# The 32 bytes of swapped gate biases in another pool, and the read of the token count behind another expert's loads

## The chip, the cores and the metric

One core of a Trainium2 chip runs the kernel. The metric is device microseconds (us) of one execution, and lower is better. TensorE does the matrix products, VectorE (DVE), ScalarE (ACT) and GpSimd (POOL) the rest, and the queue of SyncE (SP) issues nearly all transfers from the memory outside the core; 16 DMA engines carry them.

## The reference, cut to what matters

One layer over 256 tokens of width 1024: a first half with normalization, convolution and recurrence, and a mixture of 32 experts, two for each token. All is float32.

```
    x = x + g1 * (concatenate([conv_l, lru_l]) @ w_out)
    h2 = modulate(rms_norm(x, norm2_g), sh2, sc2)
    y2 = hier_moe(h2, ...)          # top 1 of 4 groups, in it the top 2 of 8 experts
    x = x + g2 * y2
    return rms_norm(x, final_g)

def swiglu_expert(xb, w1, w3, w2):  # each expert, 1024x1024 weights, on its tokens
    return (silu(xb @ w1) * (xb @ w3)) @ w2
```

The kernel reads the weights of all 32 experts: 3 matrices of 4 MB each for an expert, 403 MB in all.

## The kernel before, in words

**The stages.** The first half of the layer (the prologue, lines 97 to 852) is an order written out by hand. It works in 17 tiles named slot, each 8192 bytes in a partition, in the pool `wp`. Behind it the pool is closed and the same bytes are taken again by nine tiles named wide, each 16,384 bytes in a partition (pool `wx`). One load fills a wide with half of a weight matrix of an expert, 2048 KB: line 885, called in `up`, with 128 rows of 16,384 contiguous bytes, one for each partition. So an expert takes six loads in the order w1, w1, w3, w3, w2, w2, and the loop `for e in range(E - 1)` runs over experts 0 to 30. Loads are counted here from 0: expert e has loads 6e to 6e+5. The nine wides are taken in a fixed turn, so load n goes into the wide that load n-9 had, and SP issues it when TensorE has done its products (line 888) with load n-9. Expert 31 is loaded in shorter rows, of 2048 bytes first (line 1070).

**What TensorE does for an expert.** Sixteen products for each load; between w3 and w2 four transposes (line 1015); behind odd experts' w3 the gather of tokens for the next group of experts (line 800), behind even experts' w3 the products that add the results of the pair before (line 910).

**The token count.** The tokens of an expert fit into 64 places, or, where some expert has more, a second piece of program (`rest`) runs at the end. For this, behind expert 1, VectorE and TensorE find the greatest count (lines 1042 to 1047, result in `fmi`), and `values_load` (line 1049) reads it into a register of every engine, so that each can decide at the end whether it runs the second piece. In SP's queue this read stands where the text has it: behind the loads of expert 2 and ahead of those of expert 3. SP executes its queue in order; the read waits for `fmi`, and everything behind it waits with it.

**The biases.** `hbx`, 8 floats in each partition (32 bytes), is a copy of biases with the two halves of the partitions swapped; the activations of the recurrence's gates read it (line 425), all in the prologue. It lies in the pool `const`, which lives to the end. The pools lie one behind the other: const, the one-hot tiles, the gathered tokens (xg), the slots, tmp, big. In the built program the first slot begins at byte 66,080 of a partition, and so does the first wide, 32 bytes past a multiple of 512; the others follow at multiples of 8192 or 16,384 from there. x1, the tile that holds the tokens, lies at the head of const and begins 128 bytes past a multiple of 512.

Of the kernel before, what the change touches and what calls it, by code (L numbers as in the profile page):

```python
# [7 lines left out]
F32 = mybir.dt.float32  # L8
# [62 lines left out]
def hybrid_layer(ctx: ExitStack, tc: tile.TileContext, sp_d, x_d, c_d, bada_d, rb_d, fg_d, gw_d,  # L71
# [5 lines left out]
    const = ctx.enter_context(tc.tile_pool(name="const", bufs=1))  # L77
# [5 lines left out]
    big = pro.enter_context(tc.tile_pool(name="big", bufs=1))  # L83
    psp = ctx.enter_context(tc.tile_pool(name="psp", bufs=8, space=bass.MemoryType.PSUM))

    def bank():
        return psp.tile([128, 512], F32, name="bank")
# [136 lines left out]
    V.tensor_scalar(nkh, kh, -1.0, None, OP.mult)  # L224
    hb = sp[:, COLS["ba"][0]:COLS["bx"][1]]
    V.tensor_scalar(hb, hb, 0.5, None, OP.mult)
    hbx = const.tile([128, 8], F32, name="hbx")
    for h in range(2):
        G.tensor_copy(hbx[64 * h:64 * h + 64], hb[64 - 64 * h:128 - 64 * h, 8:16])
    dwh = col("dw")  # L230
# [313 lines left out]
    def rowbc(dst, rows, j0):  # L544
        for j in range(2):
            pr = bank()
            r = 32 * (j0 + j)
            P.matmul(pr, ones[r:r + 1, :], rows[r:r + 1, :], start=True, stop=True, tile_position=(r, 0))
            S.copy(dst[:, j * 512:(j + 1) * 512], pr)
# [230 lines left out]
    def onehot(oh, t, g):  # L780
        V.tensor_tensor(oh[:, t], iota1[:, None, :].to_broadcast([128, 4, CAP]),
                        posm[:, t, g * 4:g * 4 + 4, None].to_broadcast([128, 4, CAP]), OP.is_equal)
# [12 lines left out]
    def quad(k):  # L795

        return slice(k // 4 * 512 + k % 4, k // 4 * 512 + 512, 4)

    def gather_mm(pg, i, k, oh, t):
        P.matmul(pg[:, i * 256:(i + 1) * 256], xn[:, t, quad(k)],  # L800
                 oh[:, t].rearrange("p e s -> p (e s)"), start=t + i == 0, stop=t == 1 and i == 1,
                 skip_group_check=True)

    def gather_out(xg, pg, i, k):
        if i == 0:
            S.activation(xg[:, k], pg[:, i * 256:(i + 1) * 256], AF.Identity, scale=gsp[:, 0, k:k + 1],  # L806
                         bias=gsp[:, 1, k:k + 1])
        else:
            V.tensor_scalar(xg[:, k], pg[:, i * 256:(i + 1) * 256], gsp[:, 0, k:k + 1], gsp[:, 1, k:k + 1],  # L809
                            OP.mult, OP.add)  # L810

    def gather_new(dt=F32):
        return (ohp.tile([128, 2, 4, CAP], dt, name="oh"),
                xgt().rearrange("p (k s) -> p k s", k=8))
# [66 lines left out]
    def up(w_d, e, xs):  # L881
        ps = bank()
        for k4 in range(2):
            w = wide().rearrange("p (k n) -> p k n", k=4)
            dma(w, w_d[e, k4 * 512:(k4 + 1) * 512, :].rearrange("(p k) n -> p k n", p=128))
            for i in range(4):
                for h in range(2):
                    P.matmul(ps[64 * h:64 * h + 64, :], xs(k4 * 4 + i), w[:, i, h * 512:(h + 1) * 512],  # L888
                             start=k4 + i == 0, stop=k4 * 4 + i == 7, tile_position=(0, 64 * h))
        return ps  # L890

    def sel_build(e0):
        so = mo.tile([128, 2, 2, CAP], F32, name="so")
        for t in range(2):
            for i in range(2):
                V.tensor_scalar(so[:, t, i], iota1, posm[:, t, e0 + i:e0 + i + 1],
                                gate[:, t, e0 + i:e0 + i + 1], OP.is_equal, OP.mult)
        return so

    def sel_turn(so):  # L900
        pt = bank()
        for t in range(2):
            P.transpose(pt[:, t * 128:(t + 1) * 128], so[:, t].rearrange("p e s -> p (e s)"), ident)
        st = mo.tile([128, 256], F32, name="st")
        S.copy(st, pt[:, 0:256])
        return st

    def scatter_mm(st, yy, t, h):
        pz = bank()
        P.matmul(pz, st[:, t * 128:(t + 1) * 128], yy[:, h * 512:(h + 1) * 512], start=True, stop=True)  # L910
        return pz

    def scatter_add(pz, t, h):
        q = slice(h * 512, (h + 1) * 512)
        V.tensor_tensor(x1[:, t, q], x1[:, t, q], pz, OP.add)  # L915
# [64 lines left out]
    for e in range(E - 1):  # L980
        xs = lambda k: xg[:, k, (e % 4) * CAP:(e % 4 + 1) * CAP]
        if e % 2 == 0:
            so = sel_build(e)
        gat = e % 2 == 1 and e // 4 < E // 4 - 1
        if gat and e % 4 == 1:
            noh, nxg = gather_new()
            onehot(noh, 0, e // 4 + 1)
            onehot(noh, 1, e // 4 + 1)
        pa = up(w1_d, e, xs)
        sl = mo.tile([128, 512], F32, name="sl", bufs=1)  # L990
        S.activation(sl, pa, AF.Silu)  # L991
        if e == 0:
            rowbc(g2bc, g2r, 2)
        if e % 2 == 0:
            st = sel_turn(so)
        pb = up(w3_d, e, xs)
        gg = sl
        V.tensor_tensor(gg, sl, pb, OP.mult)  # L998
        pzs = []
        k0 = (e % 4) // 2 * 4  # L1000
        if gat:
            pgs = [bank(), bank()]
            for k in range(3):
                for t in range(2):
                    gather_mm(pgs[k // 2], k % 2, k0 + k, noh, t)
            for k in range(2):
                gather_out(nxg, pgs[0], k, k0 + k)
        elif e % 2 == 0 and e:
            for n in range(3):
                pzs.append(scatter_mm(*prev, *TH[n]))  # L1010
                if n < 2:
                    scatter_add(pzs[n], *TH[n])
        pt = bank()
        for j in range(4):
            P.transpose(pt[:, j * 128:(j + 1) * 128], gg[:, quad(j)], ident)  # L1015
        gt = mo.tile([128, 4, 128], F32, name="gt", bufs=1)
        V.tensor_copy(gt[:, 0:2], pt[:, 0:256])  # L1017
        S.copy(gt[:, 2:4], pt[:, 256:512])  # L1018
        if gat:
            for t in range(2):  # L1020
                gather_mm(pgs[1], 1, k0 + 3, noh, t)
            for k in range(2, 4):
                gather_out(nxg, pgs[1], k % 2, k0 + k)
        elif pzs:
            pzs.append(scatter_mm(*prev, *TH[3]))
            for n in range(2, 4):
                scatter_add(pzs[n], *TH[n])
        gts = lambda f: gt[:, f % 4, 64 * (f // 4):64 * (f // 4) + 64]
        py = up(w2_d, e, gts)
        if e % 2 == 0:  # L1030
            yy = mo.tile([128, D], F32, name="yy", bufs=1)
        for h in range(2):
            o = (e % 2) * 64
            V.tensor_tensor(yy[o:o + 64, h * 512:(h + 1) * 512], py[64 * h:64 * h + 64, :],  # L1034
                            g2bc[64 * h:64 * h + 64, h * 512:(h + 1) * 512], OP.mult)
        if e % 2 == 1:
            prev = (st, yy)
        if e % 4 == 3:
            xg = nxg
        if e == 1:  # L1040
            fmx = mo.tile([128, 1], F32, name="fmx")
            V.tensor_reduce(fmx, posm.rearrange("p t e -> p (t e)"), AX.X, OP.max)
            fpt = bank()
            P.transpose(fpt[0:1, 0:128], fmx, ident)
            fmr = mo.tile([1, 1], F32, name="fmr")
            V.tensor_reduce(fmr, fpt[0:1, 0:128], AX.X, OP.max)
            V.tensor_copy(fmi, fmr)
        if e == 2:
            nmax = nc.values_load(fmi[0:1, 0:1], min_val=0, max_val=T)
        if e == 2:  # L1050
            dma(fgbc[0:1, :], fg_d)
            for j in range(2):
                pr = bank()
                P.matmul(pr, ones[0:1, :], fgbc[0:1, j * 512:(j + 1) * 512], start=True, stop=True)
                S.copy(fgbc[:, j * 512:(j + 1) * 512], pr)
# [8 lines left out]
    e = E - 1  # L1064
# [171 lines left out]
```

## Time and profile before

| what | value |
| --- | --- |
| median of 3 runs | 1135.12 us (1133.21 to 1136.87) |
| the profiled execution | 1132.48 us |
| its span, first to last instruction | 1130.6 us |
| mean granted TensorE clock, as a share of 2.4 GHz | 0.983 |
| bytes moved | 445.21 MB |

The profiled execution is 2.6 us under the median. Its span leaves 1.9 us around it.

### The profile page before, as it was taken

The page shows a single profiled execution, that of the slowest core. Times are in us where ns is not written, and L with a number is a line of the kernel's source. Part 1 is how long each engine was busy: PE and PEld are TensorE (multiplying, and loading weights), DVE is VectorE, ACT ScalarE, POOL GpSimd, SP SyncE. Part 2 cuts the span into 40 slices and gives each one's busy share as a digit, 9 for nine tenths or more (in the row PEclk, how much of TensorE's full clock was granted, in tenths as well). Part 3 has the DMA queues.
Part 4 walks back from the last instruction along what each step waited for, and adds up shares of the span by engine and source line. Part 5 has one row for each costly group of instructions (what it writes and reads, how often), then busy time and mean ns, then how long its engine had stood idle before and what let it go on. Part 6 is the DMA issues. An engine that isn't in the chain of part 4 may idle for free.

```text
span 1130.6 us, 11884 instructions
## 1 busy us (share of the span) xinstructions
PE 1002.3 (89%) x4959; PEld 445.6 (39%) x4959; DVE 312.8 (28%) x632; ACT 177.1 (16%) x331; POOL 97.8 (9%) x122
## 2 busy tenths in 40 slices
PE   6898898999999888988888898888988888888896
PEld 6874547343434332333333333332323333332244
DVE  4889965211121112111211121102121211111113
ACT  4558944100100000000000000000000000000002
POOL 2667412000000000000000000000000000000001
PEclk9999898999999999999999999999999999999999
DMA  9858668989999999999999999999999999999995
GB/s 347 300 202 325 233 258 375 403 353 429 427 427 426 426 427 427 428 426 427 427 427 426 427 428 427 427 427 428 427 427 426 427 427 428 425 428 427 428 392 183
DMA packets 50015, 445.21 MB, mean 394 GB/s; under 512 B 4083, under 2 KB 14371, under 8 KB 24100
## 3 DMA queue, kind: packets, MB, share of 16 engines
q1 hardware_dynamic: 49746, 443.84, 94.3%
q8 instruction: 41, 0.67, 0.2%
q10 hardware_dynamic: 210, 0.55, 0.1%
q14 instruction: 18, 0.15, 0.0%
HBM read 443.32 MB, written 1.05 MB: 393 GB/s over the span
## 4 chain that ended last, share of the span: by engine, by line
DMA 58%; PE 32%; DVE 6%; ACT 1%; SPq 1%; issue 1%; POOL 0%; DVEq 0%; ACTq 0%
DMA wide<-in_w_dram 57%; PE bank L888 17%; PE bank L800 3%; PE bank L691 2%; PE bank L910 2%; DVE bank L480 1%; PE bank L339 1%; PE bank L385 1%; PE bank L522 1%; DVE slot L394 1%; DMA slot<-in_wada_dram 1%; PE bank L826 1%; PE bank L323 1%; PE bank L1015 1%; DVE xn L480 1%; DVE slot L298 1%
## 5 line engine op out<-in xcount | busy, mean ns | idle before, releaser
L888 PE MATMUL bank<-wide,xg 128*64 128x512 f32 x1984 | 451.9, 600 | 83.2 <-DMA wide<-in_w_dram 82.9
L888 PEld LDWEIGHTS bank<-wide,xg 128*64 128x64 f32 x1984 | 142.0, 137 | 378.4 <-issue 257.5
L888 PE MATMUL bank<-wide,gt 128*64 128x512 f32 x992 | 219.7, 595 | 1.0 <-DVE gt L1017 1.0
L998 DVE TENSOR_TENSOR sl<-sl,bank 128x512 f32<-128x512 f32 x31 | 21.3, 687 | 476.7 <-issue 452.5
L888 PEld LDWEIGHTS bank<-wide,gt 128*64 128x64 f32 x992 | 68.5, 137 | 139.9 <-issue 138.5
L1034 DVE TENSOR_TENSOR yy<-bank,g2bc 64x512 f32<-64x512 f32 x62 | 42.7, 689 | 191.4 <-PE bank L888 190.9
L991 ACT ACTIVATE sl<-bank 128x512 f32<-128x512 f32 x31 | 18.5, 597 | 436.6 <-PE bank L888 436.6
L1153 POOL TENSOR_TENSOR xg<-x,fgbc 128x256 f32<-128x256 f32 x6 | 4.3, 730 | 924.2 <-DMA wide<-in_w_dram 923.0
L800 PE MATMUL bank<-oh,xn 128*128 128x256 f32 x224 | 61.1, 416 | 0.0
L800 PEld LDWEIGHTS bank<-oh,xn 128*128 128x128 f32 x224 | 54.4, 327 | 11.4 <-issue 11.4
L910 PE MATMUL bank<-yy,st 128*128 128x512 f32 x120 | 58.0, 606 | 0.0
L1018 ACT COPY gt<-bank 128x256 f32<-128x256 f32 x31 | 11.6, 373 | 226.0 <-DVE gt L1017 226.0
L806 ACT ACTIVATE xg<-bank,gsp 128x256 f32<-128x256 f32 x32 | 17.9, 565 | 154.7 <-PE bank L800 150.1
L915 DVE TENSOR_TENSOR x<-x,bank 128x512 f32<-128x512 f32 x60 | 39.7, 683 | 7.1 <-PE bank L910 7.1
L910 PEld LDWEIGHTS bank<-yy,st 128*128 128x128 f32 x120 | 20.6, 191 | 26.5 <-issue 23.2
L339 PE MATMUL bank<-slot 128*128 128x256 f32 x192 | 26.8, 301 | 4.3 <-DVE slot L298 4.3
L809 DVE TENSOR_SCALAR xg<-bank,gsp 128x256 f32<-128x256 f32 x32 | 17.2, 543 | 47.0 <-ACT xg L806 47.0
L339 PEld LDWEIGHTS bank<-slot 128*128 128x128 f32 x192 | 25.5, 206 | 5.6 <-DVE slot L298 4.8
L311 POOL TENSOR_TENSOR slot<-slot 128x512 fp32r<-128x512 f32 x20 | 26.5, 1358 | 9.3 <-ACT slot L302 9.3
L1015 PEld LDWEIGHTS bank<-ident,sl 128*128 128x128 f32 x124 | 19.5, 203 | 11.1 <-issue 7.1
L498 POOL TENSOR_TENSOR xn<-xn,fgbc 128x256 f32<-128x256 f32 x30 | 22.6, 753 | 13.0 <-ACT fgbc L497 8.4
L385 PE MATMUL bank<-slot 128*128 128x512 f32 x96 | 22.7, 394 | 0.0
(251 smaller groups left out, 694.1 us busy)
## 6 DMA issues: line engine op xcount, KB each, us to landing
wide<-in_w_dram SPq DMA_DIRECT2D x186, 2048.0 KB, 39.2
slot<-in_wada_dram SPq DMA_DIRECT2D x16, 1024.0 KB, 7.2
slot<-in_wada_dram SPq DMA_DIRECT2D x16, 512.0 KB, 9.3
slot<-in_win_dram SPq DMA_DIRECT2D x8, 1024.0 KB, 10.2
wide<-in_w_dram SPq DMA_DIRECT2D x8, 1024.0 KB, 24.0
slot<-in_wout_dram SPq DMA_DIRECT2D x4, 1024.0 KB, 9.4
wide<-in_w_dram SPq DMA_DIRECT2D x8, 512.0 KB, 12.5
x<-in_x_dram SPq DMA_DIRECT2D x2, 512.0 KB, 4.4
```

Source lines behind the costliest of these rows:

```text
L311: en.tensor_tensor(lo[:, c:c + m], w[:, c:c + m], f(hi)[:, c:c + m], OP.subtract)
L339: P.matmul(pvg[ct][:, i * T:(i + 1) * T], wz[k // 2][wi][:, k % 2, c:c + 128], x[k // 4][:, k % 4, 0:T], start=k + i + n == 0, stop=k == 7 ...
L385: P.matmul(pu, w, x[k // 4][:, k % 4], start=k + n == 0, stop=k == 7 and n == 2)
L480: V.scalar_tensor_tensor(rows4(ypre[:, ct]) if j == 30 else y, x, w, y, OP.mult, OP.add)
L498: G.tensor_tensor(acc, acc, p, OP.add)
L691: P.matmul(p, m[:, q], w[:, c:c + 512], start=first and n == 0, stop=len(done) == 8 and n == len(passes) - 1)
L800: P.matmul(pg[:, i * 256:(i + 1) * 256], xn[:, t, quad(k)], oh[:, t].rearrange("p e s -> p (e s)"), start=t + i == 0, stop=t == 1 and i == ...
L888: P.matmul(ps[64 * h:64 * h + 64, :], xs(k4 * 4 + i), w[:, i, h * 512:(h + 1) * 512], start=k4 + i == 0, stop=k4 * 4 + i == 7, tile_positi ...
L910: P.matmul(pz, st[:, t * 128:(t + 1) * 128], yy[:, h * 512:(h + 1) * 512], start=True, stop=True)
L915: V.tensor_tensor(x1[:, t, q], x1[:, t, q], pz, OP.add)
L1015: P.transpose(pt[:, j * 128:(j + 1) * 128], gg[:, quad(j)], ident)
L1034: V.tensor_tensor(yy[o:o + 64, h * 512:(h + 1) * 512], py[64 * h:64 * h + 64, :], g2bc[64 * h:64 * h + 64, h * 512:(h + 1) * 512], OP.mult)
```

## The change

Two edits. `hbx` goes from the pool const to the pool big, which lies behind the slots and tmp. All that stood behind it in const, and the pools behind const, move down by 32 bytes: the slots and the wides then begin at multiples of 512 (the first at byte 66,048); x1 stays where it was. And `values_load` is called in the round of expert 8 and no longer in that of expert 2; `fmi` is computed where it was.

```
-    hbx = const.tile([128, 8], F32, name="hbx")
+    hbx = big.tile([128, 8], F32, name="hbx")
...
-        if e == 2:
+        if e == 8:
             nmax = nc.values_load(fmi[0:1, 0:1], min_val=0, max_val=T)
         if e == 2:
             dma(fgbc[0:1, :], fg_d)
```

SP's queue before, at the end of expert 2's loads (wide_2044 and wide_2054 are its two halves of w2, wide_2089 the first half of expert 3's w1):

```order
L885 DMA wide_2044<-in_w_dram 128x4096
L885 DMA wide_2054<-in_w_dram 128x4096
L1049 TENSOR_LOAD fmi
L1049 ISA x2
L1051 DMA fgbc<-in_fg_dram 1x1024
L885 DMA wide_2089<-in_w_dram 128x4096
L885 DMA wide_2099<-in_w_dram 128x4096
```

The same place in the changed program (the numbers of later tiles are smaller, the tiles are the same):

```order
L885 DMA wide_2044<-in_w_dram 128x4096
L885 DMA wide_2054<-in_w_dram 128x4096
L1051 DMA fgbc<-in_fg_dram 1x1024
L885 DMA wide_2075<-in_w_dram 128x4096
L885 DMA wide_2085<-in_w_dram 128x4096
```

The read and its two instructions for the bounds of the value are gone from there, and the load of the final norm's weights and expert 3's loads stand directly behind expert 2's. SP's queue in the changed program at the end of expert 8's loads:

```order
L885 DMA wide_2590<-in_w_dram 128x4096
L885 DMA wide_2622<-in_w_dram 128x4096
L885 DMA wide_2632<-in_w_dram 128x4096
L1049 TENSOR_LOAD fmi
L1049 ISA x2
L885 DMA wide_2664<-in_w_dram 128x4096
L885 DMA wide_2674<-in_w_dram 128x4096
```

Here the read now stands, 36 loads further back in the queue. TensorE's, VectorE's and ScalarE's reads move in the same way from the end of expert 2's work to the end of expert 8's. POOL's read is its next instruction after the prologue in both programs.

## Rows read from the trace of the kernel before

**Rows 1.** The page, part 2: the span in 40 slices of 28.3 us.

```profile
DMA  9858668989999999999999999999999999999995
GB/s 347 300 202 325 233 258 375 403 353 429 427 427 426 426 427 427 428 426 427 427 427 426 427 428 427 427 427 428 427 427 426 427 427 428 425 428 427 428 392 183
```

**Rows 2.** The page, part 4: the chain that ended last, by engine and line.

```profile
DMA 58%; PE 32%; DVE 6%; ACT 1%; SPq 1%; issue 1%; POOL 0%; DVEq 0%; ACTq 0%
```

**Rows 3.** The chain in order of time: start us, us, what (two stretches).

```profile
372.25 3.61 PE bank L888 x16
...
375.88 36.97 DMA wide<-in_w_dram
...
1033.98 40.01 DMA wide<-in_w_dram
```

**Rows 4.** Stretches: length, busy time (and instructions), granted clock, DMA share, GB/s.

```profile
200.00:248.00 48.00, 46.62 (x216) 18.03 (x210) 7.55 (x20) 5.88 (x13) 0.00 (x0) 1.00 1.00 426
248.00:256.00 8.00, 6.18 (x31) 2.14 (x31) 2.91 (x9) 0.00 (x0) 0.00 (x0) 1.00 0.49 168
256.00:300.00 44.00, 44.00 (x190) 17.52 (x188) 7.25 (x12) 4.51 (x9) 0.00 (x0) 1.00 1.01 427
...
376.00:700.00 324.00, 285.77 (x1244) 110.91 (x1242) 53.91 (x102) 18.76 (x39) 0.00 (x0) 1.00 1.01 427
...
1000.00:1080.00 80.00, 67.36 (x284) 22.20 (x281) 12.62 (x25) 3.06 (x7) 0.00 (x0) 0.98 1.00 426
```

**Rows 5.** What SP's queue waited for: us in total, times, longest.

```profile
SPq L885 <- DMA wide<-in_w_dram: 580.1, 141, 5.5
...
SPq L1049 <- DVE so L896: 17.7, 1, 17.7
```

**Rows 6.** What SP issued from 195 to 262 us: start us, us, what.

```profile
198.04 35.44 SPq L885 DMA_DIRECT2D wide<-in_w_dram  x10
251.61 0.31 SPq L1051 DMA_DIRECT2D fgbc<-in_fg_dram  x1
252.03 9.55 SPq L885 DMA_DIRECT2D wide<-in_w_dram  x6
```

**Rows 7.** Instructions that touch fmi: duration in ns, first and last start.

```profile
L1047 DVE CAST fmi<-fmr x1: 141/141/141, 250.6 to 250.6; 1x1 int32<-1x1 f32 x1
L1049 SPq TENSOR_LOAD <-fmi x1: 470/470/470, 250.8 to 250.8; - x1
...
L1049 PEldq TENSOR_LOAD <-fmi x1: 487/487/487, 271.3 to 271.3; - x1
L1049 DVEq TENSOR_LOAD <-fmi x1: 541/541/541, 275.8 to 275.8; - x1
```

**Rows 8.** The chain in order of time from 196 to 300 us.

```profile
215.72 20.82 PE bank L888 x96
...
241.14 7.04 PE bank L888 x32
...
250.24 7.02 PE bank L888 x32
```

**Rows 9.** TensorE in order of time about the end of expert 8.

```profile
430.37 7.09 PE L888 MATMUL bank<-wide,gt 128*64 128x512 f32 x32
437.49 3.65 PE L888 MATMUL bank<-wide,xg 128*64 128x512 f32 x16
442.33 1.08 PE L888 MATMUL bank<-wide,xg 128*64 128x512 f32 x4 [1.19 <-DMA wide<-in_w_dram]
```

**Rows 10.** The page, part 6: issues, KB each, median us from issue to landing.

```profile
wide<-in_w_dram SPq DMA_DIRECT2D x186, 2048.0 KB, 39.2
...
wide<-in_w_dram SPq DMA_DIRECT2D x8, 1024.0 KB, 24.0
```

**Rows 11.** A stretch in which expert 31's loads with rows of 2048 bytes land.

```profile
1083.00:1101.00 18.00, 15.46 (x112) 7.70 (x110) 1.80 (x3) 0.39 (x1) 0.00 (x0) 1.00 1.04 387
```

**Rows 12.** The page, part 5: two groups of VectorE, writing sl and x1.

```profile
L998 DVE TENSOR_TENSOR sl<-sl,bank 128x512 f32<-128x512 f32 x31 | 21.3, 687 | 476.7 <-issue 452.5
...
L915 DVE TENSOR_TENSOR x<-x,bank 128x512 f32<-128x512 f32 x60 | 39.7, 683 | 7.1 <-PE bank L910 7.1
```

## The prediction

> **What bounds the kernel now.** I read the page's slices first. From the tenth slice on, that is from 254 us, the core takes in 425 to 429 GB/s in every slice up to the last two, and the ninth slice, 226 to 254 us, stands out with 353 [rows 1]. The chain that ended last is more than half DMA [rows 2]. In order of time it goes through TensorE up to 375.88 us, and from there to the last expert it is the landing of loads, piece after piece of some 40 us [rows 3]. So TensorE's products end the waits before 376 us and the transfers after it. But the two are not separate stages. The stretches show that the transfers run at 426 to 427 GB/s from 200 to 248 us and again from 256 us to 1080 us, and only between, from 248 to 256 us, at 168 [rows 4]. The bytes to bring are fixed. A stream that never rests up to 1080 us ends earlier by just as much as a rest in it is shortened, also where that rest lies in a part in which TensorE was on the chain: there TensorE lived on loads that had landed, and the debt was paid at 376 us.
>
> What made the rest is in SP's queue. It issued ten loads, the last of them ending at 198.04 + 35.44 = 233.48 us, and then nothing until 251.61 us [rows 6]. The only long wait that falls there is that of the read of the token count, 17.7 us [rows 5]. The view puts it down to another VectorE instruction, but the read starts at 250.8 us, right after `fmi` is written at 250.6 us plus 0.14 [rows 7]; that is what it waited for. The first load behind it goes out at 252.03 us [rows 6].
>
> **The register read leaves expert 2's place.** What the rest costs, from the bytes: in the 8 us from 248 to 256 the stream brought 168 x 8 = 1344 KB where 427 x 8 = 3416 would have fitted; 2072 / 427 = 4.85 us [rows 4]. From the DMA share of 0.49 in the same stretch it is 8 x 0.51 = 4.1 us. I take 4.85, because the share also counts packets that are open but wait for their first bytes, and keep 4.1 as the lower end.
>
> Does the rest go away whole, or is the wait for the read followed by a wait for a free wide? Load 18, the first of expert 3, needs the wide of load 9, the last half of expert 1's w3. TensorE is done with it at 215.72 + 20.82 = 236.54 us. Loads 10 and 11 are the 32 products from 241.14 us, so they are done at 244.7 and 248.2 us, and load 12 is the first half of the 32 from 250.24 us, done at 253.8 [rows 8]. A load of 2048 KB takes 2,097,152 / 427,000 = 4.91 us of the stream [rows 4, 10]. The stream comes to load 18 at 248 us at the earliest, to 19, 20 and 21 at 252.9, 257.8 and 262.7 us. SP can issue them at 236.5, 244.7, 248.2 and 253.8: 8 to 11 us ahead each, against the rest's 252.03 us now. After that TensorE frees a wide in 7.04 / 2 = 3.5 us of products, 4.3 us with the other work of an expert counted (29 loads' products from 250.24 to 375.86 us) [rows 3, 8], and the stream needs 4.91 to fill one, so the distance grows. What is late next in SP's queue is the landing of the load before: it already makes up its longest sum of waits, 580.1 us [rows 5], and a wait of SP that leaves loads in flight costs nothing. So the whole 4.85 us goes.
>
> The load of the final norm's weights, 4 KB, goes out some 15 us sooner and is used at the end of expert 2's work as before; 0.31 us of SP's time [rows 6], nothing on the stream.
>
> **The read behind expert 8's loads.** `fmi` is then ready for more than 150 us and no engine waits for it. SP spends 252.03 - 250.8 = 1.2 us on the read, its two checks and the small load [rows 6, 7], and less without the last. At that place loads take 39.2 us from issue to landing [rows 10], which at 4.91 us is eight loads in flight: 1.2 us late in issuing is covered by all but the last of them. Without that cover it would cost 1.2 us, once. TensorE reads for 0.49 us and VectorE for 0.54 [rows 7]. TensorE's read comes between expert 8's last product and expert 9's first, at 437.49 us; the next load's products start at 442.33 us after 1.19 us of waiting for DMA [rows 9], so a delay of 0.49 us disappears in that wait. VectorE and ScalarE wait for TensorE there. Taken at zero; the end of the range for it is 0.5 us.
>
> **The 32 bytes.** No instruction is added or removed; the same copy fills `hbx`. What changes is where tiles begin. For the engines, the trace has the same VectorE form on a tile that begins 32 bytes past a multiple of 512 and on one that begins 128 past it: 687 and 683 ns [rows 12], no difference to speak of, and neither of them is on the stream's path. Taken at zero.
>
> For the transfers no row shows a destination at a multiple of 512, so I bound it. A row of 16,384 bytes on one of 16 engines takes 16,384 x 16 / 427 = 613.9 ns [rows 4], a row of 2048 bytes 2048 x 16 / 387 = 84.7 ns [rows 11]. Straight through both: 0.0369 ns for a byte and 9.1 ns for each row whatever its length. All rows begin 32 bytes past, so if the start costs anything, it is within these 9.1 ns. A load has 8 rows for each engine, and there are 186 [rows 10]: 9.1 x 8 x 186 = 13.5 us, and 256 rows more of 2048 bytes for each engine in eight loads of 1024 KB, 2.3 us. So the gain lies between 0 and 15.8 us; from the other side, a loss of the same size is the farthest that I allow, since no row excludes it. I take 0: it is nearest to the engines' rows above, and any transfer in rows has to pay something for each row, wherever it begins.
>
> One rule speaks for a value between. The Trainium skill, "DMA: Bandwidth & Descriptors", section "How a descriptor splits into AXI transactions", says that transactions start at multiples of 256 bytes, and that a transfer starting between them carries unused bytes ahead of its start in its first one, which still cost. The page tells it of what is fetched; here the side that moves is the one written, and no run here shows it. By the row the sum stays as it is, and what the rule would make of it is the first of the rivals.
>
> **The sum.** -4.85 us for the read, 0 for the rest. The profiled execution's 1132.48 us would be 1127.6. It ran 2.6 us under the median of the runs shown, so on the median 1135.12 - 4.85 = 1130.3 us.
>
> **The rivals.**
> *One beat a row.* If each row lost the time of the 32 bytes by which it is off, 32 x 0.0369 = 1.2 ns, the aligned start would give 1.2 x 8 x 186 = 1.8 us more: 1128.5 us. For it: a row's fixed 9.1 ns has room for it. Against: rows of 16,384 and 2048 bytes fit a cost that has nothing to do with the start as well. This is what the skill's rule named above would make of it. Chance 0.15.
> *The start is the row's whole fixed cost.* 15.8 us more: 1114.5 us. Against: then rows would have no other cost at all. Chance 0.05.
> *The rest is given back.* A later wait takes up the 4.85 us, as where SP waits for a wide that TensorE frees late. For it: TensorE is on the chain up to 376 us. Against: the 8 to 11 us worked out above, and no later stretch under 426 GB/s up to 1080 us. 1135 us, chance 0.08.
> *Slower.* Writes that begin at a multiple of 512 cost more in a row, for instance because they now meet TensorE's reads of another wide, which begin alike. It decides from 4.85 us / (8 x 186) = 3.3 ns a row, 427 GB/s falling to 424.7; at 9.1 ns it gives 1130.3 + 15.8 = 1146 us. Against: the wides already lie 16,384 bytes apart, so they began alike before, too. Chance 0.05.
>
> **How the numbers follow.** The forecast has 0.67. Its own range is 1130.3 to 1131.0 from the two readings of the rest, 1131.5 with half a microsecond for the read, and the runs of before spread by 1.8 us to either side. The case of one beat ends at 1128.5 - 1.8 = 1126.7. So 1126.5 to 1133 us; the case of 1114.5, that of 1135 and the slower one, 0.18 together, are left out. A measurement of this kernel tells about 0.3%, 3.4 us, from no change. The forecast is 1.4 us beyond that, so of its 0.67 I put 0.09 down to the middle. Faster: 0.58 + 0.15 + 0.05 = 0.78; same: 0.08 + 0.09 = 0.17; slower 0.05.
>
> **What the changed profile would show.** SP's wait at line 1049 is gone or under a microsecond; loads go out between 236 and 252 us; the stretch from 248 to 256 us is at 420 GB/s or more; TensorE leaves the chain for the transfers later than 376 us, since the stream is further ahead. The reads stand between 385 and 440 us and nobody waits for them. If the start of a tile matters, the stretch from 376 to 700 us is not at 427 GB/s: one beat makes it 428, the whole row cost 433. I am wrong if the stretch at 250 us fills and another empties, or if the rate moves by more than a gigabyte a second.

## The result, and the profile after

| what | before | after |
| --- | --- | --- |
| median | 1135.8 us (4 runs) | 1121.17 us (1118.39 to 1122.21, 4 runs) |
| ratio, 95% interval | | 0.9871 [0.9845, 0.9896] |
| the profiled execution, its span | 1132.48, 1130.6 us | 1120.63, 1118.8 us |

The kernel became 14.6 us faster where 4.85 was forecast. The direction was right; the time lies outside the range, and 0.67 of the chances stood on a sum that was a third of the gain.

The page's slices of the changed kernel, of 28.0 us each, against [rows 1]:

```profile
DMA  9766759899999999999999999999999999999995
GB/s 360 253 246 248 279 209 431 373 431 431 431 431 431 431 430 430 431 431 431 431 431 431 430 431 430 431 430 431 430 431 431 431 430 431 431 431 431 431 409 193
```

The ninth slice is no longer a hole, as forecast. But all slices behind it, up to the last two, also stand at 430 or 431 GB/s, where before none passed 429. The stretches, against [rows 4] (same columns):

```profile
200.00:248.00 48.00, 46.62 (x216) 18.34 (x217) 9.14 (x25) 7.52 (x16) 0.00 (x0) 1.00 0.98 413
248.00:256.00 8.00, 6.18 (x31) 1.99 (x29) 2.91 (x9) 0.00 (x0) 0.00 (x0) 1.00 1.00 429
256.00:300.00 44.00, 44.00 (x190) 17.52 (x188) 7.25 (x12) 4.51 (x9) 0.00 (x0) 1.00 1.01 431
...
376.00:700.00 324.00, 294.58 (x1286) 114.38 (x1284) 56.28 (x108) 18.76 (x39) 0.00 (x0) 0.99 1.01 431
```

From 248 to 256 us the stream now brings 429 GB/s where it brought 168. From 256 us on it runs at 431 and not at 427. What SP issued, against [rows 6]:

```profile
157.62 78.00 SPq L885 DMA_DIRECT2D wide<-in_w_dram  x18
235.68 0.33 SPq L1051 DMA_DIRECT2D fgbc<-in_fg_dram  x1
238.73 21.05 SPq L885 DMA_DIRECT2D wide<-in_w_dram  x5
```

Load 18 goes out at 238.73 us and no longer at 252.03. That is as soon as TensorE has freed its wide, by the end of the products with loads 4 to 9 in the chain:

```profile
217.87 20.82 PE bank L888 x96
```

No wait at line 1049 is left in the list of SP's waits. The reads of the token count, against [rows 7] (the view of one line, durations in ns, first and last start):

```profile
L1049 SPq TENSOR_LOAD <-fmi x1: 499/499/499, 392.1 to 392.1; - x1
...
L1049 PEldq TENSOR_LOAD <-fmi x1: 487/487/487, 428.6 to 428.6; - x1
```

And TensorE about the end of expert 8, against [rows 9]:

```profile
425.98 7.09 PE L888 MATMUL bank<-wide,gt 128*64 128x512 f32 x32
432.92 3.65 PE L888 MATMUL bank<-wide,xg 128*64 128x512 f32 x16
437.75 2.79 PE L888 MATMUL bank<-wide,xg 128*64 128x512 f32 x12 [1.17 <-DMA wide<-in_w_dram]
```

Nothing stands still at the read: TensorE's begins at 428.6 us, while its products of expert 8 still run. The second load of expert 9 keeps its products waiting 1.17 us for DMA, 1.19 before. The chain in order of time, in the changed kernel and against [rows 3]:

```profile
200.29 7.02 PE bank L888 x32
...
399.75 3.61 PE bank L888 x16
...
403.37 34.33 DMA wide<-in_w_dram
...
1074.25 15.16 DMA wide<-in_w_dram
...
1089.43 12.83 DMA wide<-in_w_dram
```

and the same in the kernel before, its first products and the end of the stream:

```profile
197.97 7.18 PE bank L888 x32
...
1083.90 16.70 DMA wide<-in_w_dram
...
1100.61 13.44 DMA wide<-in_w_dram
```

TensorE leaves the chain at 403 us and no longer at 376, since the stream is further ahead. Where the 11.8 us between the two spans went can be read off: the first expert's products begin 2.3 us later than before in this execution (200.29 against 197.97 us); from there to the loads with short rows it takes 1074.25 - 200.29 = 873.96 us instead of 1083.90 - 197.97 = 885.93, so 12.0 us less; and those loads take 27.99 us instead of 30.14, 2.2 us less. The 12.0 us is more than twice the 4.85 that were worked out for the read.

### The profile page after: what moved, and what is told of

The parts are those of the page before. It is cut to its first block, busy times and chain, and to the rows that moved or that the text cites. A ratio compares the mean times of both kernels' runs of the same rounds, so it can differ in the third digit from the quotient of the medians.

```text
span 1118.8 us, 11884 instructions
## 1 busy us (share of the span) xinstructions
PE 1002.7 (90%) x4959; PEld 447.1 (40%) x4959; DVE 313.3 (28%) x632; ACT 177.2 (16%) x331; POOL 97.9 (9%) x122
## 4 chain that ended last, share of the span: by engine, by line
DMA 53%; PE 36%; DVE 7%; issue 1%; SPq 1%; ACT 0%; POOL 0%; DVEq 0%; ACTq 0%
DMA wide<-in_w_dram 53%; PE bank L888 20%; PE bank L800 3%; PE bank L910 2%; PE bank L691 2%; PE bank L339 2%; DVE bank L480 1%; PE bank L385 1%; DVE slot L394 1%; PE bank L522 1%; PE bank L826 1%; DVE slot L298 1%; PE bank L1015 1%; PE bank L323 1%; DVE slot L297 1%; DVE xn L480 1%
## 5 line engine op out<-in xcount | busy, mean ns | idle before, releaser
L339 PE MATMUL bank<-slot 128*128 128x256 f32 x192 | 29.2, 315 | 9.4 <-DVE slot L298 7.7
L311 POOL TENSOR_TENSOR slot<-slot 128x512 fp32r<-128x512 f32 x20 | 26.7, 1365 | 11.8 <-DMA slot<-in_wada_dram 8.8
## 6 DMA issues: line engine op xcount, KB each, us to landing
wide<-in_w_dram SPq DMA_DIRECT2D x8, 512.0 KB, 11.8
```

What stands on the lines that cost most here:

```text
L311: en.tensor_tensor(lo[:, c:c + m], w[:, c:c + m], f(hi)[:, c:c + m], OP.subtract)
L339: P.matmul(pvg[ct][:, i * T:(i + 1) * T], wz[k // 2][wi][:, k % 2, c:c + 128], x[k // 4][:, k % 4, 0:T], start=k + i + n == 0, stop=k == 7 ...
```

## The experiments

All ratios are to the kernel before on the same chip, with their 95% intervals. A stretch that is compared is that from 376 to 700 us unless another is named.

**One part alone.** e1 takes the second edit of the diff and leaves the first; e2 the other way round.

> The read behind expert 8's loads, the biases in const as before (slots and wides 32 bytes past a multiple of 512). Theory 'two parts': the read is worth the rest in the stream alone, 4.85 us: ratio to before 0.9957, the stretch at 250 us filled, the stream still at 427 GB/s in the stretch from 376 us on. Rival 'one cause' (filling the rest is what lets the stream run faster, the biases do nothing): as the changed kernel, ratio 0.987 and 431 GB/s.

> The biases moved, the read in expert 2's place. Theory 'two parts': a start at a multiple of 512 takes 5.3 ns off each row of 16,384 bytes and 4.0 ns off each row of 2048, 5.3 x 8 x 186 + 4.0 x 256 = 8.9 us: ratio 0.992, the stream at 431 GB/s, and the rest at 250 us still there with about 170 GB/s in its 8 us. Rival 'one cause': ratio 1.000 and 427 GB/s.

e1: 1130.53 us, 0.9955 [0.9936, 0.9974]. Its stretches:

```profile
248.00:256.00 8.00, 6.18 (x31) 1.99 (x29) 2.91 (x9) 0.00 (x0) 0.00 (x0) 1.00 1.00 427
...
376.00:700.00 324.00, 289.62 (x1266) 112.62 (x1264) 53.94 (x102) 18.74 (x39) 0.00 (x0) 1.00 1.01 427
```

e2: 1126.93 us, 0.9917 [0.9888, 0.9946]. In its profiled execution the experts begin later, so the rest lies from 253 us on:

```profile
253.00:261.00 8.00, 6.18 (x31) 2.00 (x29) 2.91 (x9) 0.00 (x0) 0.00 (x0) 1.00 0.43 146
261.00:300.00 39.00, 39.00 (x167) 15.07 (x164) 5.97 (x10) 3.57 (x7) 0.00 (x0) 1.00 1.01 432
...
376.00:700.00 324.00, 289.10 (x1259) 112.45 (x1259) 55.66 (x106) 19.14 (x40) 0.00 (x0) 1.00 1.01 431
```

The read alone fills the rest and leaves the stream at 427 GB/s; the biases alone leave the rest and raise the stream to 431 to 432. The two multiply to 0.9955 x 0.9917 = 0.9872, the changed kernel's 0.9871; that they agree so closely is luck, since each interval is some 2 us or more to either side. So there are two causes, and they add up within the noise. "One cause" falls.

**Wides or slots.** In e3 and e4 an unused tile ahead of the wides moves them and not the slots, by 120 floats (in e1's kernel, from 32 bytes past to a multiple of 512) or by 8 (in the changed kernel, the other way):

```
     wx = ctx.enter_context(tc.tile_pool(name="wx", bufs=1, reuse_waits="tile"))
...
+    wx.tile([128, 120], F32, name="pad")   # e4: 8 floats, in the changed kernel
     turn = [0]
```

> The read behind expert 8's loads, the biases in const, and 480 bytes of an unused tile ahead of the wides: slots 32 bytes past, wides at a multiple of 512. Theory 'rows of the wides': the saving is in the rows that land in the wides, so this is the changed kernel again: ratio 0.987, 431 GB/s. Rival 'slots' (the first half of the layer, or the move of the biases, brings part of it): nearer to 0.9957, or 427 GB/s.

> As the changed kernel, with 32 bytes of an unused tile ahead of the wides: slots at a multiple of 512, wides 32 bytes past. Theory 'rows of the wides': as the read alone, ratio 0.9957, 427 GB/s. Rival 'slots': 0.987, or at least below 0.993.

The times do not decide: e3's 1131.15 us, 0.9967 [0.9949, 0.9984], is nearer to what the rival said, and e4's 1142.21 us, 1.0052 [1.0033, 1.0071], fits neither. The rates do. e3 and then e4, the stretch at the end of the first half and the long one:

```profile
160.00:180.00 20.00, 19.06 (x66) 11.04 (x65) 5.66 (x9) 4.45 (x12) 4.10 (x9) 1.00 0.43 161
...
376.00:700.00 324.00, 289.21 (x1246) 111.21 (x1245) 54.60 (x103) 18.20 (x38) 0.00 (x0) 0.99 1.01 431
```

```profile
160.00:180.00 20.00, 20.00 (x65) 11.27 (x65) 7.55 (x12) 3.78 (x10) 3.91 (x6) 1.00 0.33 120
...
376.00:700.00 324.00, 286.94 (x1230) 108.60 (x1227) 55.43 (x104) 17.61 (x37) 0.00 (x0) 0.99 1.01 427
```

The stream follows the wides: 431 with them on a multiple, 427 with them off it, whatever the slots do. The times are spoilt by the pad. Moved against the slots, a wide lies over three slots instead of two, and its first load waits for the third as well: SP's wait ahead of a first load is 17.1 us for a slot of line 445 in e3, where e1 has 12.0 us for one of line 311 (e3's line, then e1's, and e1's stretch at the end of the first half):

```profile
SPq L886 <- DVE slot L445: 17.1, 1, 17.1
```

```profile
SPq L885 <- DVE slot L311: 12.0, 1, 12.0
```

```profile
160.00:180.00 20.00, 19.56 (x67) 11.04 (x65) 6.80 (x12) 3.95 (x11) 4.22 (x9) 1.00 1.01 430
```

From 160 to 180 us e1 brings 430 GB/s, e3 161; at 430 that is 12.5 us lost, and 367 against 428 in the next 20 us and 421 against 431 in the 48 behind give 2.8 and 1.1 back: 8.6 us, just about what the faster rows are worth. For e4 the same sum (120, 426 and 427 GB/s) is 14.4 - 2.7 - 0.7 = 11.0 us, and it is 11.7 over e1. These sums account for the times after the event; no run tests them.

**Which multiple.** Here small tiles of the first half follow `hbx` behind the slots, so slots and wides move together and no wide lies over a third slot:

```
-    th = const.tile([128, 16], F32, name="th")
+    th = big.tile([128, 16], F32, name="th")       # e7; e5: th, kh and lw; e6: mod_a
```

> As the changed kernel, with three more small tiles of the first half moved behind the slots (256 bytes): slots and wides begin 256 bytes past a multiple of 512. Theory 'multiples of 256': as the changed kernel, ratio 0.987 and 431 GB/s. Rival 'multiples of 512': as the read alone, 0.9957 and 427 GB/s.

> As the changed kernel, with one more tile of 128 bytes moved behind the slots: slots and wides begin 384 bytes past a multiple of 512, a multiple of 128 but not of 256. Theory 'multiples of 256' and rival 'multiples of 512': as the read alone, 0.9957 and 427 GB/s. Rival 'multiples of 128': as the changed kernel, 0.987 and 431 GB/s.

> As the changed kernel, with one more tile of 64 bytes moved behind the slots: slots and wides begin 448 bytes past a multiple of 512, a multiple of 64 alone. Theories 'multiples of 256', of 128 and of 512: as the read alone, 0.9957 and 427 GB/s. Rival 'multiples of 64' (only the 32 bytes matter): 0.987 and 431 GB/s. If the cost grows with the bytes past the start, this is slower than the read alone.

e5: 1121.37 us, 0.9865 [0.9847, 0.9883]. e6: 1127.69 us, 0.9939 [0.9922, 0.9956]. e7: 1130.09 us, 0.995 [0.9931, 0.9968]. Their long stretches, e5 first:

```profile
376.00:700.00 324.00, 294.59 (x1278) 114.86 (x1280) 57.63 (x108) 19.11 (x40) 0.00 (x0) 0.99 1.01 430
```

```profile
376.00:700.00 324.00, 290.18 (x1270) 112.83 (x1268) 54.68 (x104) 18.74 (x39) 0.00 (x0) 1.00 1.01 428
```

```profile
376.00:700.00 324.00, 290.30 (x1270) 113.06 (x1268) 55.54 (x105) 18.74 (x39) 0.00 (x0) 1.00 1.01 428
```

A start 256 bytes past a multiple of 512 is as good as a multiple; 128 and 192 past a multiple of 256 cost as the 32 do, or 1 GB/s less. The bytes of the trace's packets, summed over this stretch, tell it finer: a row of 16,384 bytes takes 608.8 ns with the start on a multiple of 256 (after, e2, e3, e5), and 614.1, 613.0 and 613.1 ns with it 32, 128 and 192 bytes past (e1, e6, e7). So it is multiples of 256, and the cost does not grow with how far past them the row begins. The Trainium skill, "DMA: Bandwidth & Descriptors", section "How a descriptor splits into AXI transactions", has transactions begin at multiples of 256 bytes, and the multiple that these runs show is the same. The page says so of bytes fetched and counts the unused bytes ahead of the start as the price; in these runs the side off the multiple is the one written, and 192 bytes past cost no more than 32, so that price is not the one measured here.

**Does TensorE have a part in it.** e8 and e9 multiply a quarter of each load:

```
-            for i in range(4):
+            for i in range(1):
...
-                             start=k4 + i == 0, stop=k4 * 4 + i == 7, tile_position=(0, 64 * h))
+                             start=k4 == 0, stop=k4 == 1, tile_position=(0, 64 * h))
```

> The read behind expert 8's loads, wides 32 bytes past; of each load of experts 0 to 30 only the first of four slices of 128 is multiplied, so TensorE reads a quarter of each wide. Theory 'the write alone': 427 GB/s all the same, the cost sits in the transfer's rows. Rival 'writes meet TensorE's reads': with a quarter of the reads three quarters of the 4 GB/s come back, 430 GB/s.

> As the run before, wides at a multiple of 512 (the changed kernel with a quarter of the products). Theory 'the write alone': 431 GB/s, about 8.9 us less than its partner. Rival 'writes meet TensorE's reads': within 2 us of its partner.

e8: 1126.47 us, 0.99 [0.987, 0.9931], e9: 1117.15 us, 0.9819 [0.9789, 0.985]; e8 first:

```profile
376.00:700.00 324.00, 175.20 (x454) 61.60 (x454) 54.89 (x106) 19.31 (x39) 0.00 (x0) 0.64 1.01 427
```

```profile
376.00:700.00 324.00, 176.95 (x458) 61.74 (x458) 54.89 (x106) 19.28 (x39) 0.00 (x0) 0.64 1.01 431
```

427 and 431 GB/s and 9.3 us between the two, with TensorE's reads of the wides down to a quarter. By the packets' bytes the start costs 5.2 ns a row here and 5.3 with all of the reads. So the cost sits in the transfer, and TensorE's reads have no part in it that could be told.

**Four times as many rows.** e10 and e11 cut each row of 16,384 bytes into four rows of 4096:

```
-            dma(w, w_d[e, k4 * 512:(k4 + 1) * 512, :].rearrange("(p k) n -> p k n", p=128))
+            dma(w, w_d[e, k4 * 512:(k4 + 1) * 512, :].rearrange("(k p) n -> p k n", p=128))
```

> The read behind expert 8's loads, wides 32 bytes past, and experts 0 to 30 loaded in rows of 4096 bytes, four for each that there was (the products then multiply other rows of the weights with each token's slice, so the sums differ). By the line through 16,384 and 2048 bytes a row of 4096 takes 0.0369 x 4096 + 9.1 = 160.2 ns: 409 GB/s, some 39 us longer than the read alone.

> As the run before, wides at a multiple of 512 (the same part is changed). Theory 'a cost for each row': four times as many rows, so four times the saving: 4.0 to 5.3 ns x 32 x 186 = 24 to 32 us less than its partner, 419 to 423 GB/s. Rival 'a share of the bytes' (0.9% faster whatever the row): 9 us less, 413 GB/s.

e10: 1170.46 us, 1.0286 [1.0249, 1.0322]. e11: 1141.78 us, 1.0056 [1.0036, 1.0076]; e10 first:

```profile
376.00:700.00 324.00, 275.03 (x1191) 104.29 (x1191) 53.33 (x101) 17.04 (x36) 0.00 (x0) 1.00 1.02 409
```

```profile
376.00:700.00 324.00, 284.52 (x1232) 109.31 (x1229) 52.38 (x99) 17.36 (x37) 0.00 (x0) 0.99 1.02 421
```

The line through the two lengths of [rows 4, 11] gave 409 GB/s for rows of 4096 bytes, and it is 409. The start is worth 1170.46 - 1141.78 = 28.7 us here where it is worth 1136.45 - 1126.93 = 9.5 in e2 (against the kernel before beside it). A share of the bytes would have given the 9.5 again. So it is a cost for each row; it came to three times and not four, since a shorter row loses a little less (the table below).

**Is a part given back in the first half.** In all eight profiles with the slots on a multiple of 256 bytes the first expert's products begin at 199.7 us or later; with the slots off it they begin at 197.7 to 198.6 us in five of seven, and at 201.4 and 201.7 in e8 and e10. e12 moves the second group of GpSimd's subtractions to VectorE, and e13 is the changed kernel again.

```
-ZH, ZL = "SSSS", "GGGG"
+ZH, ZL = "SSSS", "GVGG"
```

> The changed kernel, with the subtractions for the second quarter of w_in (line 311) on VectorE and not on GpSimd. Theory 'a part is given back': with slots at a multiple of 512 the loads of the first 40 us land sooner, GpSimd's second group of subtractions falls on VectorE's modulation (lines 297 and 298, 1.36 us an operation while GpSimd works, 0.42 us else), and the first expert begins 2 us or more later than with slots 32 bytes past. Then this begins the experts at about 198 us where the changed kernel's profile has 200.3, and its ratio is near 0.985. Rival 'only the clock at the start' (the later start is how this one execution's clock fell): no sooner than the changed kernel run beside it, or slower, by VectorE's 3.4 us more of work.

> The changed kernel itself, on the same chip as the run before: ratio 0.987; by theory 'a part is given back' its experts begin at 200 us or later again, by the rival at 198 us as often as not.

e12: 1120.95 us, 0.9873 [0.9849, 0.9896]; e13: 1120.31 us, 0.9868 [0.9844, 0.9892]. VectorE in order of time (start us, us), e13 and then e12:

```profile
33.60 1.37 DVE L298 TENSOR_TENSOR slot<-slot 128x256 fp32r<-128x256 f32 x1
34.89 1.36 DVE L297 TENSOR_SCALAR slot<-slot,g1s,mod_a 128x256 f32<-128x256 f32 x1
```

```profile
32.57 0.43 DVE L298 TENSOR_TENSOR slot<-slot 128x256 fp32r<-128x256 f32 x1
32.91 0.41 DVE L297 TENSOR_SCALAR slot<-slot,g1s,mod_a 128x256 f32<-128x256 f32 x1
```

GpSimd in e13 at that time:

```profile
31.91 5.47 POOL L311 TENSOR_TENSOR slot<-slot 128x512 fp32r<-128x512 f32 x4 [0.23 <-ACT slot L302]
```

The meeting of the two engines is real, and e12 removes this one and not the others: 1.36 us becomes 0.42 here. But the first expert begins at 199.77 us in e12 and at 200.31 in e13, not at 198, and the medians differ by 0.6 us the other way. So the theory is not borne out. e12 also gives VectorE the subtractions to do, so what the slow operations alone cost is not separated. They stand in the profile of the kernel before too, whose experts begin at 197.97 us. Why the experts begin later in these profiles stays open.

## Why the prediction was right and where it was wrong

*The rest and its size.* Right. SP's long wait is gone, loads go out from 238.73 us on, the stretch fills, and the read alone is worth 0.0045 x 1136 = 5.1 us (3.0 to 7.3 by its interval) where 4.85 was worked out. Nothing took the place of the wait.

*The read behind expert 8.* Right: nothing waits for it.

*Given back.* Right to give it little: from 248 us on the stream does not rest again, and e1's gain is whole within its interval.

*The 32 bytes, for the transfers.* This is the step that failed, a term put at nothing: "I take 0: it is nearest to the engines' rows above, and any transfer in rows has to pay something for each row, wherever it begins." The second half is true: in e11, with all rows on a multiple, a row of 4096 bytes takes 155.7 ns, and 0.0369 x 4096 is 151.1. But of the 9.1 ns that each row pays, about half was the start. From the rates of before (and e10) off the multiple and of after (and e11) on it:

| row, bytes | off the multiple | on it | saved a row |
| --- | --- | --- | --- |
| 16,384 | 427 GB/s, 614.1 ns | 431 GB/s, 608.8 ns | 5.3 ns |
| 4096 (e10, e11) | 409 GB/s, 160.2 ns | 421 GB/s, 155.7 ns | 4.5 ns |
| 2048 (expert 31) | 387 GB/s, 84.7 ns | 406 GB/s, 80.7 ns | 4.0 ns |

The last 406 is this row of the changed kernel, against [rows 11]:

```profile
1074.00:1089.00 15.00, 14.18 (x104) 7.01 (x100) 1.79 (x3) 0.39 (x1) 0.00 (x0) 1.00 1.05 406
```

Whole gigabytes leave a nanosecond or more open in the first line, so there the packets' bytes were summed from 376 to 700 us: 426.85 and 430.57 GB/s. With it the term is 5.3 x 8 x 186 + 4.0 x 256 = 8.9 us, inside the bounds of 0 and 15.8 that the step had set; e2 measured 0.0083 x 1136 = 9.4 (6.1 to 12.7 by its interval). With the read's 4.85 it makes 13.8 of the 14.6, and what is left is within the noise. The engines' rows, on which the value was chosen, said nothing about a transfer. The rival with one beat was a fifth of the right size, the one with the whole fixed cost 1.8 times the right size. Both bounds were known, nothing in the trace told which was nearer, and then the range should have run through the whole of them, down to 1114 us.

*What should have shown it wrong* did: the rate of the stretch from 376 us, named there with 427, 428 and 433, came out at 431.

*Slower.* It did not come: starts on the multiple made the stream faster in e2. Nor do writes and TensorE's reads meet at a price that depends on the start: with a quarter of the reads, in e8 and e9, the difference between the starts stays what it was.

## What to carry to other kernels

Where a kernel lives on its transfers, let the tiles that they fill begin at multiples of 256 bytes; it costs no more than another order of allocation, and the shorter the rows the more it brought here (1% of the rate at 16 KB, 3% at 4 KB, 5% at 2 KB). A register read in the queue that issues loads holds up every load behind it, so place it where its value has long been ready; what it costs is the hole in the transfers, not the wait that stands in the list. And when the trace gives only bounds for a term, the range is the bounds.

## What the runs showed of the hardware that was not expected

A row that begins off a multiple of 256 bytes in the on-chip memory costs 4.0 to 5.3 ns more on its DMA engine when it is 32 bytes past, and no more when it is 128 or 192 past (4.2 and 4.3 ns at 16,384 bytes). What in the transfer takes this time no run shows. And VectorE's operations on 128x256 float32 take 1.36 us while GpSimd subtracts beside them and 0.42 us else; taking one of their meetings away, at the price of more work for VectorE, made no difference that the runs could tell (1120.95 us against 1120.31).
